# Cached attention in a decoder trunk: values behind the first query block, the merge in four parts, query copies shared, a residual load moved

## The chip, the cores and the metric

The kernel runs on one core of a Trainium2 chip. The metric is the device time of one execution in microseconds (us). Five engines work side by side, each through its own instructions in a fixed order: TensorE (PE, matrix products; its weight loads are listed as PEld), VectorE (DVE), ScalarE (ACT), GpSimd (POOL) and SyncE (SP), which issues transfers. Transfers are also issued from ACT and POOL. Engines wait for each other through semaphores.

## The reference, cut to what matters

The program is one inference step of a two-layer decoder: 1024 new prompt tokens and 8 sample tokens, one for each cached sequence. Layer 0 mixes with an mLSTM, layer 1 with latent attention of 8 heads, and each layer ends in a SwiGLU network. The change lies in layer 1's attention and in the output projection behind it.

```python
def mla_attend_prompt(q_lat, q_rope, c_kv, k_r):          # 1024 tokens, causal
    ...
        s = einsum('bqhc,bkc->bhqk', ql, c_kv) + einsum('bqhr,bkr->bhqk', qr, k_r)
        s = where(kpos <= qpos, s * MLA_SCALE, -inf)
        p = softmax(s)
        return einsum('bhqk,bkc->bqhc', p, c_kv)

def mla_attend_sample(...):                               # 8 sequences, 8192 cached rows each
    c_all = concatenate([cache_latent[layer_idx, pages].reshape(past, KV_LORA), cn])
    kr_all = concatenate([cache_k_rope[layer_idx, pages].reshape(past, QK_ROPE), krn])
    s = einsum('qhc,kc->hqk', ql, c_all) + einsum('qhr,kr->hqk', qr, kr_all)
    p = softmax(s * MLA_SCALE)
    return einsum('hqk,kc->qhc', p, c_all)
```

A cached row has 256 latent and 64 rotary float32 values; the pages lie scattered, and a table gives their order. After the attention comes the output projection, `hp + y @ w_o`, the sum of squares of the result, and the next network.

## The kernel before, in words

All products are float32, made of three products of split operands (high x high, high x low, low x high).

**Order of the work.** The kernel is written as a program for a planner that runs ahead of time. Each instruction has a priority from its place in the program; the planner walks through a cost model's time and gives each engine, among the instructions that its model says are ready, the one of highest priority. What it decides is a fixed order for each engine. `high_priority(offset=SOON)` moves instructions ahead in that choice, and `issue_after(x)` says that instructions of x's engine stand behind x in its order; it is a lower limit, and nothing else is tied by it. On the chip, an engine that reaches an instruction whose operands are missing stands still, with all behind it.

**Attention** (`attention`, from L1594). There are 32 slots: 8 heads by 4 groups G of 256 query rows. In a slot `prompt(h, G)` works on two query blocks of 128 rows. For each block it makes the scores in banks `sc` (L1697 to L1702), ends with a product that adds the causal mask (L1704), takes the maximum (L1705), the exponentials (L1714) and the scaling (L1719). Then, for both blocks, come the transposes of the probabilities (L1737), their split, and the products with the values (L1757), and the result is copied to `ot` (L1760) and stored (L1762). `head_ops` makes the next head's keys and values between the slots; its key products are tied behind `self.qk`, the last mask product.

**The samples' stream** runs beside it. After most slots one unit of `sample_units` is written: a unit gathers 2048 cached rows with indirect transfers on POOL's queue (L1849 into `nat`, four buffers; L1850 into `nrp`, two), transposes them on DVE (L1857) and makes scores (L1864). Two units are a half of a sequence; 16 halves are 8 sequences. After the second unit come maximum, exponentials, a transpose, and 16 copies of the probabilities into `pz` (L1885), eight on DVE and eight on ACT. The rest of the half is the function `values` (L1888), stored in `self.due`: 64 products of the probabilities with the gathered rows (L1893), which free the two `nat` buffers, and the update of the accumulator `acc` (L1894). After a sequence's second half it also merges the 16 partial results of each head: a transpose of the maxima (L1898), a maximum and a broadcast (L1900, L1902), a product that spreads it (L1903), factors (L1905, L1906, L1907), a product that adds up the sums (L1908), weights (L1910, L1912) and the products that give the output (L1914, L1915). The next slot's `prompt` calls it in one go, between its softmax and its transposes, and the 64 products are tied behind `self.qk`, the mask product of the second block.

**The samples' queries** (`sample_query`, L1552) are made once, ahead of the stream: 16 copies of 32x128 on ACT (L1574) and eight of 32x64 on DVE (L1576) put them in `qbd`.

**The output projection** (`out_proj`, `op_tile`). Half 0 is 512 tokens, half 1 is 520. For each half eight tiles d of 128 outputs are made from 24 products; the residual X is added (L871), squared on ACT, and the squares are summed in SS, on POOL for d = 1 to 6 and on DVE for d = 7 (L877). A tile's weights are loaded on SP's queue (L142) and split on ACT and DVE (L117, L118). `op_residual` loads a half of the residual as eight transfers (L843): half 0 on SP's queue ahead of the tiles, half 1 on POOL's queue behind tile d = 0.

Of the kernel before, what the change touches and what calls it, by code (L numbers as in the profile page):

```python
# [13 lines left out]
ALU = mybir.AluOpType  # L14
# [4 lines left out]
P = 128  # L19
D = 1024  # L20
KT = D // P
# [70 lines left out]
class Kern:  # L92
# [764 lines left out]
    def op_tile(self, i, d, tags, early=None):  # L857
# [5 lines left out]
        for cs in OPC[i]:  # L863
# [8 lines left out]
            if d == 0:  # L872
                nc.scalar.activation(SS[:, cs], x, AF.Square)
            else:
                sq = self.t(self.sq[i], [P, 512], "sq")[:, :m]
                nc.scalar.activation(sq, x, AF.Square)  # L876
                (V if d == KT - 1 else nc.gpsimd).tensor_tensor(SS[:, cs], SS[:, cs], sq, op=ALU.add)  # L877
# [3 lines left out]
    def out_proj(self, layer):  # L881
# [672 lines left out]
    def sample_query(self, tq, wT):  # L1554
# [16 lines left out]
        for kb in range(4):  # L1571
            d = qbd[32 * kb:32 * kb + 32, :, :, 8 * kb:8 * kb + 8]
            for cq in range(4):
                nc.scalar.copy(d[:, :, cq:8:4], ql[32 * cq:32 * cq + 32].rearrange("p f (h b) -> p b f h", b=NS))  # L1574
# [19 lines left out]
    def attention(self, ckh, ckl, kk, kl, cqp, cq):  # L1594
# [17 lines left out]
        self.due = None  # L1612
# [59 lines left out]
        def prompt(h, G, kt, vt):  # L1672
# [10 lines left out]
            for i in (2 * G, 2 * G + 1):  # L1683
# [8 lines left out]
                for c in range(nb):  # L1692
# [10 lines left out]
                    if last:  # L1703
                        self.qk = mm(o[:, w - P:], mk[:, 0], mk[:, 1], start=False, stop=True).ins  # L1704
# [18 lines left out]
            if self.due:  # L1723
                self.due()
            for j0 in range(0, nk, 4):
# [3 lines left out]
                for j2 in range(0, m, 2):  # L1729
# [3 lines left out]
                    for jj in range(2):  # L1733
                        for i in range(2):
                            if diag and jj == 1 and i == 0:
                                continue
                            nc.tensor.transpose(ps[:, jj, i * P:(i + 1) * P], pn[i][:, (j + jj) * P:(j + jj + 1) * P], self.ident)  # L1737
# [40 lines left out]
        for h in range(8):  # L1778
# [11 lines left out]
            for i, G in enumerate(range(4) if h % 2 == 0 or h == 7 else range(3, -1, -1)):  # L1790
# [8 lines left out]
                if slot == 30:  # L1799
                    next(units, None)  # L1800
                    if self.due:
                        self.due()
# [19 lines left out]
    def sample_units(self, b, first):  # L1822
# [6 lines left out]
        if self.due:  # L1829
            self.due()  # L1830
# [57 lines left out]
        def values():  # L1888
            self.due = None
# [5 lines left out]
            if not first:  # L1895
                m = t([P, 1], "m", 1)
                V.tensor_scalar(m, nb, -1.0, None, op0=ALU.mult)
                nc.tensor.transpose(ss[0:1, 0:P], m, self.ident)  # L1898
# [4 lines left out]
                nc.tensor.matmul(ss[:, P:P + 1], mc.rearrange("o x h -> o (x h)"), self.ones[0:1, 0:1], start=True, stop=True)  # L1903
# [4 lines left out]
                nc.tensor.matmul(ss[:, 256:257], self.ct[:, C_SL:C_SL + P], lrow, start=True, stop=True)  # L1908
# [4 lines left out]
                for f in range(2):  # L1913
                    nc.tensor.matmul(ss[:, 384 + f * 8:392 + f * 8], acc[:, f * P:(f + 1) * P], w, start=True, stop=True)  # L1914
# [167 lines left out]
```

## Time and profile before

| | us |
|---|---|
| median of three runs | 2600.45 (2599.62 to 2604.7) |
| profiled execution | 2597.15 |
| its span | 2595.3 |
| PE busy | 2492.7 (96%) |
| DVE busy | 1859.5 (72%) |
| ACT busy | 1328.1 (51%) |
| POOL busy | 573.6 (22%) |
| attention with the samples' stream | about 1330 to 1800 |
| output projection of layer 1 | about 1798 to 1903 |

Times in the profile count from the span's start. A group row gives line, engine, operation, tiles and shapes. A wait row reads: engine, tile and line that waited, what ended the wait, then the total in us, the number of waits and the longest. A timeline row gives start and duration in us, and in brackets the idle time of the engine ahead of it with what ended it; an engine name with a trailing q is its queue. A stretch's row gives its length, the busy time of each engine with the number of instructions, the granted clock of TensorE as a share of full speed, the share of the transfer engines and GB/s.

### The profile page before, as it was taken

How to read it: one execution, taken by the hardware profiler on the slowest of the kernel's cores; microseconds unless marked ns; L12 is line 12 of the kernel's file. 1: busy time of each engine (PE TensorE's matmuls, PEld its weight loads, DVE VectorE, ACT ScalarE, POOL GpSimd, SP SyncE). 2: the span in 40 equal slices, each digit the busy share in tenths (PEclk: the TensorE clock that was granted, in tenths of full speed). 3: DMA queues.
4: the chain of work that ended last, by engine and by line, in shares of the span. 5: the costliest groups of instructions: out<-in, count | busy, mean ns of one | idle time of the engine just before them, and what ended most of it. 6: DMA issues, size and time to landing. Idle time of an engine off the chain costs nothing.

```text
span 2595.3 us, 54269 instructions
## 1 busy us (share of the span) xinstructions
PE 2492.7 (96%) x21151; PEld 2360.5 (91%) x21151; DVE 1859.5 (72%) x4491; ACT 1328.1 (51%) x3281; POOL 573.6 (22%) x588
## 2 busy tenths in 40 slices
PE   8998988999999999999988898999999999999998
PEld 8998987999999999999986767777899999999998
DVE  4345669898777777766658777778498877777765
ACT  4122334456655556554454555656256656556643
POOL 1000102301111111112435555542211111111102
PEclk9999999999999999999988999999999999999999
DMA  5123545526566666555467676664535666665663
GB/s 194 42 63 85 151 143 123 162 75 135 117 129 128 127 126 120 111 151 172 157 241 282 232 250 236 222 242 152 192 106 114 119 127 128 130 129 115 120 136 118
DMA packets 343127, 382.87 MB, mean 148 GB/s; under 512 B 23465, under 2 KB 275502, under 8 KB 334550
## 3 DMA queue, kind: packets, MB, share of 16 engines
q0 software_dynamic: 58688, 180.35, 29.9%
q1 hardware_dynamic: 258982, 182.30, 23.7%
q10 hardware_dynamic: 25200, 16.75, 2.4%
q8 instruction: 166, 2.72, 0.4%
q14 instruction: 91, 0.75, 0.1%
HBM read 253.63 MB, written 125.70 MB: 146 GB/s over the span
## 4 chain that ended last, share of the span: by engine, by line
PE 69%; DVE 9%; DMA 6%; issue 2%; ACT 2%; POOL 2%; SPq 0%; ACTq 0%; POOLq 0%; DVEq 0%
PE sc L134 13%; PE sc L136 13%; PE sc L135 13%; PE mm L134 5%; PE mm L136 5%; PE mm L135 5%; DMA nat<-in_cache_latent_dram,idx 2%; PE ss L134 2%; PE ss L135 2%; PE ss L136 2%; DVE tt L1857 2%; PE ss L1864 2%; PE ss L1893 1%; DVE wl L118 1%; PE mm L1757 1%
## 5 line engine op out<-in xcount | busy, mean ns | idle before, releaser
L1187 POOL DMA_DIRECT2D x_d<-wl x72 | 86.8, 1205 | 996.8 <-DVE wl L1186 359.3
L117 ACT ACTIVATE wh<-wr 128x512 fp32r<-128x512 f32 (+2 forms) x167 | 133.5, 800 | 193.8 <-PE mm L135 114.4
L1857 DVE STREAM_TRANSPOSE tt<-nat 128x1024 f32<-128x1024 f32 x128 | 155.4, 1228 | 28.9 <-DMA nat<-in_cache_latent_dram,idx 24.3
L118 DVE TENSOR_TENSOR wl<-wr,wh 128x1024 fp32r<-128x1024 f32 (+2 forms) x80 | 92.5, 1158 | 37.6 <-ACT wh L117 36.2
L134 PE MATMUL mm<-zh,wh 128*128 128x344 f32 x320 | 104.1, 325 | 6.1 <-DVE ot L467 6.1
L117 ACT ACTIVATE b<-u 128x256 fp32r<-128x256 f32 (+1 forms) x252 | 98.5, 415 | 20.4 <-PE ss L136 6.3
L118 DVE TENSOR_TENSOR b<-u,b 128x256 fp32r<-128x256 f32 (+1 forms) x252 | 102.9, 422 | 6.8 <-ACT b L117 5.4
L1187 POOL DMA_DIRECT2D x_d<-st x72 | 105.0, 1459 | 4.2 <-DVE dC L118 3.8
L136 PE MATMUL mm<-zh,wl 128*128 128x344 f32 x320 | 103.7, 324 | 0.0
L135 PE MATMUL mm<-zl,wh 128*128 128x344 f32 x320 | 103.7, 324 | 0.0
L118 DVE TENSOR_TENSOR wh<-S,wh 128x512 fp32r<-128x512 f32 x108 | 74.5, 689 | 34.6 <-ACT wh L117 34.3
L1864 PE MATMUL ss<-tt,qbd 128*32 128x128 f32 x2560 | 88.1, 280 | 10.9 <-DVE tt L1857 8.9
L1864 PEld LDWEIGHTS ss<-tt,qbd 128*32 128x32 f32 x2560 | 70.5, 112 | 26.4 <-DVE tt L1857 18.5
L117 ACT ACTIVATE wh<-S 128x512 fp32r<-128x512 f32 x108 | 67.9, 629 | 44.3 <-PE sc L136 32.1
L134 PE MATMUL sc<-zh,wh 128*128 128x344 f32 x256 | 82.8, 324 | 0.2 <-DVE q L432 0.2
L1757 PE MATMUL mm<-wh,vt 128*128 128x256 f32 (+1 forms) x320 | 74.7, 297 | 8.4 <-ACT wh L117 7.1
L136 PE MATMUL sc<-zh,wl 128*128 128x344 f32 x256 | 82.1, 321 | 0.2 <-DVE wl L118 0.2
L135 PE MATMUL sc<-zl,wh 128*128 128x344 f32 x256 | 82.1, 321 | 0.0
L1714 ACT ACTIVATE wr<-sc,mx,rqt 128x512 f32<-128x512 f32 (+2 forms) x96 | 64.5, 676 | 30.1 <-DVE mx L1709 14.9
L1850 POOL DMA_INDIRECT nrp<-in_cache_k_rope_dram,idx x64 | 61.4, 959 | 57.9 <-DVE tt L1857 24.5
L877 POOL TENSOR_TENSOR ss<-ss,sq 128x512 f32<-128x512 f32 (+2 forms) x36 | 50.7, 1407 | 106.0 <-ACT sq L876 106.0
L1757 PEld LDWEIGHTS mm<-wh,vt 128*128 128x128 f32 x320 | 56.0, 198 | 18.1 <-ACT wh L117 11.2
(1078 smaller groups left out, 10659.1 us busy)
## 6 DMA issues: line engine op xcount, KB each, us to landing
wr<-in_ffn_w_gate_up_dram SPq DMA_DIRECT2D x96, 512.0 KB
x_d<-st POOLq DMA_DIRECT2D x72, 520.0 KB, 7.8
x_d<-wl POOLq DMA_DIRECT2D x72, 512.0 KB, 5.9
dr<-in_ffn_w_down_dram SPq DMA_DIRECT2D x72, 256.0 KB
wr<-in_mlstm_w_in_dram SPq DMA_DIRECT2D x24, 512.0 KB
wr<-in_mlstm_w_out_dram SPq DMA_DIRECT2D x16, 512.0 KB
q<-qn_d SPq DMA_DIRECT2D x28, 256.0 KB
wr<-in_mla_w_o_dram SPq DMA_DIRECT2D x14, 512.0 KB
```

Source lines behind the costliest of these rows:

```text
L117: ins = nc.scalar.activation(hi, src, AF.Copy)
L118: self.low = e.tensor_tensor(lo, src, hi.bitcast(F32), op=ALU.subtract)
L134: mm(ps, wh, xh, start=start, stop=False, **kw)
L135: mm(ps, wh, xl, start=False, stop=False, **kw)
L136: self.last = mm(ps, wl, xh, start=False, stop=stop, **kw)
L877: (V if d == KT - 1 else nc.gpsimd).tensor_tensor(SS[:, cs], SS[:, cs], sq, op=ALU.add)
L1187: nc.gpsimd.dma_start(self.x_d[:, 2 * dp:2 * dp + 2, 512 * i:512 * i + 2 * PW[i]], st[i], accum_op=ALU.add)
L1714: nc.scalar.activation(px[:, ks], o, AF.Exp, bias=mx[:, 0:1], scale=f, accum_out=sm[:, c:c + 1])
L1757: nc.tensor.matmul(o, x, y, start=i == 0, stop=i == len(ops) - 1)
L1850: nc.gpsimd.indirect_dma_start(out=nrp[:, s].rearrange("p s c -> p (s c)"), out_offset=None, in_=rop, in_offset=ix)
L1857: V.transpose(out=tt, in_=src.rearrange("p s (c i) -> p c s i", i=32))
L1864: nc.tensor.matmul(psS[32 * j:32 * j + 32, u * P:u * P + P], self.qbd[:, b, cb], tt[:, c, 4 * j:4 * j + 4].rearrange("p s k -> p (s k)"), ...
```

## The change

It has three parts. First, `values` becomes a generator of four pieces: `prompt` runs one behind the softmax, one ahead of the products with the values, one in the middle of them, and what is left at their end. `self.qk` is now the mask product of the first block of a slot. The pieces' PE steps are tied behind that mark, behind the last transpose, behind the middle product and behind the last product. Where a unit starts with a generator still open, it is run to its end at once. Second, every other of the 16 query copies goes to DVE. Third, the residual's half 1 is loaded behind tile d = 3 in place of d = 0, and its transfers are tied behind POOL's sum of that tile.

```diff
-                (V if d == KT - 1 else nc.gpsimd).tensor_tensor(SS[:, cs], SS[:, cs], sq, op=ALU.add)
+                self.sqa = (V if d == KT - 1 else nc.gpsimd).tensor_tensor(SS[:, cs], SS[:, cs], sq, op=ALU.add)
...
-                if d == 0:
-                    self.op_residual(1, nc.gpsimd)
+                if d == 3:
+                    with self.tc.issue_after(self.sqa.ins):
+                        self.op_residual(1, nc.gpsimd)
...
-                nc.scalar.copy(d[:, :, cq:8:4], ql[32 * cq:32 * cq + 32].rearrange("p f (h b) -> p b f h", b=NS))
+                (nc.scalar.copy, V.tensor_copy)[cq % 2](d[:, :, cq:8:4], ql[32 * cq:32 * cq + 32].rearrange("p f (h b) -> p b f h", b=NS))
...
-                        self.qk = mm(o[:, w - P:], mk[:, 0], mk[:, 1], start=False, stop=True).ins
+                        qk = mm(o[:, w - P:], mk[:, 0], mk[:, 1], start=False, stop=True).ins
+                        self.qk = qk if i % 2 == 0 else self.qk
...
-            if self.due:
-                self.due()
+            next(self.due, None)
...
-                            nc.tensor.transpose(ps[:, jj, i * P:(i + 1) * P], ...)
+                            self.tn = nc.tensor.transpose(ps[:, jj, i * P:(i + 1) * P], ...)
...
+            next(self.due, None)
             for i, (o, x, y) in enumerate(ops):
-                nc.tensor.matmul(o, x, y, start=i == 0, stop=i == len(ops) - 1)
+                self.pv = nc.tensor.matmul(o, x, y, start=i == 0, stop=i == len(ops) - 1)
+                if i == len(ops) // 2:
+                    next(self.due, None)
+            drain(self.due)
...
         def values():
-            self.due = None
...
             if not first:
                 m = t([P, 1], "m", 1)
                 V.tensor_scalar(m, nb, -1.0, None, op0=ALU.mult)
-                nc.tensor.transpose(ss[0:1, 0:P], m, self.ident)
+                with self.tc.high_priority(offset=SOON), self.tc.issue_after(self.qk):
+                    nc.tensor.transpose(ss[0:1, 0:P], m, self.ident)
+                yield
...
-                nc.tensor.matmul(ss[:, P:P + 1], mc.rearrange("o x h -> o (x h)"), self.ones[0:1, 0:1], start=True, stop=True)
+                with self.tc.issue_after(self.tn.ins):
+                    nc.tensor.matmul(ss[:, P:P + 1], mc.rearrange("o x h -> o (x h)"), self.ones[0:1, 0:1], start=True, stop=True)
+                yield
...
-                nc.tensor.matmul(ss[:, 256:257], self.ct[:, C_SL:C_SL + P], lrow, start=True, stop=True)
+                with self.tc.issue_after(self.pv.ins):
+                    nc.tensor.matmul(ss[:, 256:257], self.ct[:, C_SL:C_SL + P], lrow, start=True, stop=True)
+                yield
...
-                for f in range(2):
-                    nc.tensor.matmul(ss[:, 384 + f * 8:392 + f * 8], acc[:, f * P:(f + 1) * P], w, start=True, stop=True)
+                with self.tc.issue_after(self.pv.ins):
+                    for f in range(2):
+                        nc.tensor.matmul(ss[:, 384 + f * 8:392 + f * 8], acc[:, f * P:(f + 1) * P], w, start=True, stop=True)
...
-        self.due = values
+        self.due = values()
```

More of the change, by code (lines that the diff above doesn't have):

```diff
@@ L1611, in attention @@
         ahead = {}
-        self.due = None
+        self.due = iter(())
         def load_q(h, G):
@@ L1736, in prompt @@
                                 continue
[L1737 removed]
+                            self.tn = nc.tensor.transpose(ps[:, jj, i * P:(i + 1) * P], pn[i][:, (j + jj) * P:(j + jj + 1) * P], self.ident)
                     if diag:
@@ L1800, in attention @@
                     next(units, None)
-                    if self.due:
-                        self.due()
+                    drain(self.due)
                     pr.release()
@@ L1828, in sample_units @@
         rop = self.cache_k_rope.rearrange("l n (r s) c -> (l n r) (s c)", s=8)
-        if self.due:
-            self.due()
+        for _ in self.due:
+            pass
         if first:
```

1 line of the change is left out of this document (removed).

## The prediction

> **What bounds the kernel now.** I read the page's first part, then a table of busy time over stretches, then who waited for whom inside the stretch that the change touches.
>
> ```profile
> PE 2492.7 (96%) x21151; PEld 2360.5 (91%) x21151; DVE 1859.5 (72%) x4491; ACT 1328.1 (51%) x3281; POOL 573.6 (22%) x588
> ...
> core 0: us, PE busy (x) PEld busy (x) DVE busy (x) ACT busy (x) POOL busy (x), PEclk, DMA share, GB/s
> 1330.00:1800.00 470.00, 418.34 (x5245) 335.02 (x5245) 351.10 (x782) 268.13 (x705) 221.32 (x219) 0.95 0.67 233
> ...
> 1475.90:1479.30 3.40, 3.40 (x16) 3.24 (x15) 3.40 (x10) 1.22 (x5) 0.00 (x0) 0.50 0.98 387
> 1837.70:1841.10 3.40, 2.91 (x7) 2.15 (x7) 2.36 (x3) 1.69 (x2) 1.38 (x1) 0.50 0.31 90
> ```
>
> TensorE (PE) is the bound: 96% busy. It leaves 102.6 us of the span, and half of that, 470 - 418.3 = 51.7 us, lies in 1330 to 1800, the cached attention that the change edits. VectorE (DVE) is busy 351 of 470 us there, so it is no second bound. The last two rows show what a pause costs besides itself: 3.4 us at half the granted clock (0.50), each behind a pause of some three microseconds (both are quoted below as waits of 3.0 and 3.11). Half of 3.4 us, 1.7 us, is lost each time.
>
> ```profile
> PE ss L1864 <- DVE tt L1857: 8.9, 7, 2.6
> ...
> PE sc L1697 <- ACT wr L1714: 6.6, 4, 5.5
> PE ss L1903 <- DVE sS L1902: 5.4, 4, 3.0
> PE mm L134 <- ACT ot L1760: 4.7, 2, 2.6
> ...
> PE mm L1737 <- ACT wr L1719: 2.2, 5, 1.1
> PE ss L1914 <- DVE w L1912: 1.8, 3, 0.8
> PE ss L1903 <- DVE tt L1857: 1.3, 1, 1.3
> ```
>
> These are PE's waits in that stretch (total us, times, longest). The pauses are many and small. Those of the merge (L1903, L1914) sum to 8.5 us.
>
> **Part A, the second residual half.** The eight POOL loads of 260 KB go from behind tile d=0 to behind POOL's sum of tile d=3.
>
> ```profile
> 1827.11 8.81 DMA wr<-in_mla_w_o_dram
> ...
> 1817.75 4.34 POOL L843 DMA_DIRECT2D x<-x_d  x8 [5.03 <-DVE wl L118]
> 1829.94 1.29 POOL L877 TENSOR_TENSOR ss<-ss,sq 128x512 f32<-128x512 f32 x1 [1.18 <-ACT sq L876]
> ...
> 1837.12 0.50 PE L134 MATMUL mm<-zh0h,wh 128*128 128x512 f32 x1 [3.11 <-ACT wh L117]
> 1838.38 0.79 PE L136 MATMUL mm<-zh0h,wl 128*128 128x512 f32 x1 [0.49 <-DVE wl L118]
> 1855.76 0.28 PE L134 MATMUL mm<-zh1h,wh 128*128 128x256 f32 x1
> ...
> DMA packets 5678, 6.95 MB, mean 289 GB/s; under 512 B 368, under 2 KB 3630, under 8 KB 5678
> q0 software_dynamic: 640, 2.13, 23.4%
> ```
>
> The weights of tile d=5 take 8.81 us to land, and PE stands 3.11 + 0.49 = 3.6 us, then runs at half clock (1.7): 5.3 us. The last two rows are of 1816 to 1840: 6.95 MB went through, of which POOL's queue, the second residual half, was 2.13 MB, or 7.4 us at the mean 289 GB/s. Without it ahead, the weights land some 5 us earlier and the stall goes. The moved loads leave after POOL's fourth row, at about 1831, take 4.3 us to issue, and are first needed when PE finishes the tile begun at 1855.76: over 20 us of cover. Late next could be the weights of d=6, asked for just then: at worst their stall replaces this one (gain 0). Nothing that POOL does then waits behind the new wait except its sums of d=4 to d=6, and issuing cost them 4.34 us at the old place as well. Bounds: 0 to 5.3; being nearest to the upper row, I take **4.5**.
>
> **Part C, query copies.** Eight of sixteen copies leave ScalarE (ACT) for DVE.
>
> ```profile
> L1574 ACT COPY qbd<-ql x16: 413/416/428, 1338.6 to 1347.2; 32x128 f32<-32x128 f32 x16
> L1576 DVE COPY qbd<-qrS x8: 208/215/420, 1321.8 to 1325.3; 32x64 f32<-32x64 f32 x8
> L1885 DVE COPY pz<-pT x128: 140/186/1296, 1383.4 to 1779.2; 32x64 f32<-32x64 f32 x128
> ...
> 1348.65 0.67 ACT L1714 ACTIVATE wr<-sc,mx,rqt 128x384 f32<-128x384 f32 x1 [1.04 <-issue]
> 1349.44 0.16 DVE L1717 RECIPROCAL sm<-sm 128x1 f32<-128x1 f32 x1 [6.10 <-ACT wr L1714]
> 1353.43 1.29 POOL L130 TENSOR_TENSOR wl<-spl,wh 128x512 fp32r<-128x512 f32 x1 [13.99 <-ACT spl L129]
> 1354.88 0.98 POOL L1850 DMA_INDIRECT nrp<-in_cache_k_rope_dram,idx  x1 [0.15 <-DVE mx L1709]
> ```
>
> The exponentials at 1348.65 wait behind the copies on ACT; PE waits 5.5 us for them (the first L1697 row above), and POOL stands 14 us on ACT's split with the next gather queued behind it. Eight copies off ACT are 8 x 0.416 = 3.3 us. On DVE a copy of twice the elements of L1576 costs 0.19 to 0.43 us, so at most 3.4 us, under DVE's 6.1 us of idling at the same place. PE's wait, ACT's split and the gather all move up by 3.3. Bounds: the worst DVE copy of the rows is 1.296 us, and eight of those, 10.4 us, would outlast the 6.1 by 4.3 (a loss of 4.3); at the other end stand 5.0 gained (3.3 and one half-clock stretch). The median row being the nearest, I take **3.3**.
>
> L1885's row, 186 ns at the median and 1296 at the most, shows that DVE's copies are now and then held up for a microsecond. The Trainium skill, "SBUF — State Buffer", section "SBUF: two separate sides", names a cause that would work both ways: an fp32 copy within SBUF on VectorE and GpSimd's accesses exclude each other at a shared port, and GpSimd cannot write the descriptors of its own DMAs meanwhile. The trace agrees as far as the copies go; no row here shows a gather held up. By that rule part C would be 0 and the sum 11.2, by the row it is 3.3 and 14.5.
>
> **Part B, values and merge.** The value products (L1893) were ordered behind the second query block's last score product; now behind the first's. The merge's four PE steps, once issued in one go, are tied behind the scores, the transposes, the middle and the end of the prompt's value products.
>
> ```profile
> 1454.80 0.24 ACT L1885 COPY pz<-pT 32x64 f32<-32x64 f32 x1
> 1460.45 0.85 PE L1893 MATMUL ss<-nat,pz 128*32 128x256 f32 x12
> ...
> 1526.26 0.38 PE L1903 MATMUL ss<-ones,sS 1*128 1x1 f32 x2 [1.07 <-DVE sS L1902]
> ...
> 1701.79 0.24 ACT L1885 COPY pz<-pT 32x64 f32<-32x64 f32 x1
> 1702.04 0.22 PE L1704 MATMUL sc<-mk 128*128 128x128 f32 x1
> ...
> 1712.43 0.31 PE L1704 MATMUL sc<-mk 128*128 128x128 f32 x1
> 1712.67 3.66 PE L1893 MATMUL ss<-nat,pz 128*32 128x256 f32 x64
> 1716.11 0.96 POOL L1849 DMA_INDIRECT nat<-in_cache_latent_dram,idx  x1 [0.16 <-issue]
> ...
> 1738.91 0.22 PE L1704 MATMUL sc<-mk 128*128 128x128 f32 x1
> 1743.78 0.42 PE L1893 MATMUL ss<-nat,pz 128*32 128x256 f32 x4
> ...
> DVE tt L1857 <- DMA nat<-in_cache_latent_dram,idx: 24.3, 10, 6.6
> POOL nat L1849 <- PE ss L1893: 13.5, 6, 6.4
> POOL acc L1833 <- PE ss L1914: 6.8, 3, 3.0
> ```
>
> In the group at 1712 the last copy of the probabilities ends at 1702.03 and the first block's last product at 1702.26; the values start at 1712.67, right after the second block's. So 10.4 us are free to be taken, and the gather that refills the freed buffers goes out only at 1716.11. Ten of the sixteen groups are held so, by 1.8 to 10.4 us; the first (copies done at 1455.04, values at 1460.45) and the last (first block done at 1739.13, values at 1743.78) stand in the fence. The last three rows say why it matters: POOL waits 13.5 us for these products before gathering, and DVE then waits 24.3 us for the data, which reaches PE as the 8.9 us of L1864.
>
> - Merge waits: 8.5, of which the merge behind slot 11 (the row at 1526, 1.07), where two units follow each other with no prompt between them, stays in one go. Of the 7.4 left I take two thirds, **5.0**; bounds 0 to 9 with one half-clock stretch.
> - Earlier gathers: of L1864's 8.9, 2.6 are the very first gather, so 6.3 can go; the waits for the prompt's store (ot, 4.7) may go too if the store no longer meets the burst of gathers. I take half of the 11.0, **5.7** with a little clock; bounds 0 to 14.4 (both whole, and two half-clock stretches).
> - Lost cover: the 3.66 us of values ran while the second block's softmax was made. PE already waits 2.2 us for that (L1737). Scores of the cache and products of the next head can fill in, but not always: **-4.0**, bounds 0 to -36.6 (ten groups, nothing fills).
> - The next head's key products hang on the same mark and are freed too: no instruction more, fillers for the pauses. I cost them at nothing; badly placed they are part of the lost cover.
> - Queue: POOL's clear of the accumulator waits for the last merge product (6.8 us, three times), now tied behind the prompt's last value product; gathers and POOL's splits queue behind it. I put it inside the -4.0.
>
> Sum of B: **6.7**. A + B + C = 14.5. The profiled execution took 2597.15 (span 2595.3 and 1.85 around it), 3.3 under the median 2600.45; it would become 2582.65, the median **2586**.
>
> **The rivals.**
> 1. *Lost cover decides* (slower). Place: between the second block's mask product and its transposes. At 1712.43 the values gave 3.66 us; if other work fills only 1.5 of it, PE loses 2.16 x 10 = 21.6 us. The gathers bring nothing then, as their data is no longer what is waited for, and 12.8 of A, C and the merge remain: 8.8 slower, 2609. It decides once more than 1.3 us a group (12.8 / 10) stays open. For: the 2.2 us row. Against: PE had fillers ready around 1716 (cache scores), and the planner places values by when it reckons them ready.
> 2. *Nothing measurable.* The pauses move rather than go: C is eaten by the wait for the first gather (2.6 us of L1864), the merge's waits reappear at the tied places, and of A some 3.5 stays: 2597.
> 3. *All of it goes.* A 5.3, C 5.0, merge 7.4, half of the rest 7.3: 25 faster, 2575.
> 4. *The change doesn't do what it says.* The tie is a lower limit only; if the planner still places the values after the second block, B gives nothing: 14.5 - 6.7 = 7.8, 2592.6.
> 5. *DVE's copies hold up POOL's gathers*: eight copies of 0.43 us are 3.4 us in which the gathers at 1335 to 1355 could not be issued, as much as ACT gains, so C is 0: 2589.3. For: the 1296 ns. Against: POOL stood idle for 14 us there, so there was little to hold up. The Trainium skill's "SBUF — State Buffer" has this rule, as said under part C.
>
> **How the numbers follow.** Forecast 0.43, rival 1 0.12, 2 0.16, 3 0.12, 4 0.12, 5 0.05. A difference of 0.2% is 5.2 us. Faster: 0.43 + 0.12 + 0.12 + 0.05 = 0.72; same 0.16; slower 0.12. The range holds rivals 2 to 5 with their scatter and stops short of rival 1's centre: 2573 to 2606. The forecast's own case alone spans 2580 to 2591.
>
> **What would show it.** A: the pause before tile d=5 is gone and that stretch has full clock. C: ACT's exponentials near 1348 start 3 us earlier, with DVE's eight copies at 0.2 to 0.43 us. B: value products start after an odd-numbered mask product with the second block's scores behind them; waits on L1902 and L1912 fall under 2 us together; DVE's 24.3 us on the gathers falls by half. I am wrong if PE's waits for L1719 or L117 grow by more than 10 us, if the stretch from 1330 to 1800 is not shorter by at least 5 us, or if the weights of d=6 inherit the stall.

## The result, and the profile after

The changed kernel takes **2634.14 us** (median, 2629.25 to 2636.95); the kernel before, measured beside it, 2601.81. The ratio is **1.0123** [1.0103, 1.0142]: 32 us slower, where 15 us faster was forecast. The profiled execution took 2631.37 us, with a span of 2629.6.

The first part of the page after, and the stretch of the cached attention (columns as before):

```profile
PE 2505.1 (95%) x21151; PEld 2371.1 (90%) x21151; DVE 1859.5 (71%) x4499; ACT 1322.2 (50%) x3273; POOL 573.5 (22%) x588
```

```profile
1330.00:1800.00 470.00, 400.73 (x4888) 321.44 (x4887) 320.36 (x719) 241.34 (x634) 218.93 (x216) 0.91 0.65 228
```

PE executes the same 21151 products. In the same 470 us it got through 4888 of them instead of 5245; its pauses grew from 51.7 to 69.3 us, and the granted clock fell from 0.95 to 0.91. Since the count is equal, the start of the n-th product after can be set against that of the n-th before (times below are those before). The profiled run after is already 4.3 us late when the attention begins, though nothing is changed there; some 4 us ahead in slot 11, at 1519; 14 late at 1603, 23 at 1665, 39 at 1800; and 33.4 late from 1890 to the end. So the loss lies in slots 12 to 31, where prompt slots and cache units run side by side. PE's waits after, in 1325 to 1850:

```profile
PE ss L1868 <- DVE tt L1861: 17.0, 10, 5.1
PE sc L1698 <- DMA q<-qn_d: 13.6, 5, 6.9
PE mm L1738 <- ACT wr L1721: 12.7, 6, 5.0
...
PE sc L1698 <- ACT wr L1716: 3.9, 5, 1.7
PE sc L134 <- ACT zh0h L117: 3.7, 1, 3.7
```

The merge's 8.5 us are off the list, and L1698's wait for the exponentials fell from 6.6 to 3.9. In their place the cache scores wait for transposed keys 17.0 us (8.9 before, L1864), the transposes for scaled probabilities 12.7 (2.2 before, L1737), and the scores for the prompt's queries 13.6, which was no wait at all before. VectorE's waits in the same stretch:

```profile
DVE tt L1861 <- DMA nat<-in_cache_latent_dram,idx: 32.1, 10, 8.3
DVE fac L1912 <- PE ss L1909: 23.2, 6, 9.2
...
DVE rl L1919 <- PE ss L1916: 9.1, 5, 3.9
```

The wait for gathers did not halve; it rose from 24.3 to 32.1. The merge's waits have moved to VectorE (23.2 for the spread product), where the transposes of the next keys queue behind them. PE around slot 21, after:

```profile
1686.49 0.28 PE L1705 MATMUL sc<-mk 128*128 128x128 f32 x1
1686.70 3.66 PE L1896 MATMUL ss<-nat,pz 128*32 128x256 f32 x64
1690.29 0.50 PE L1698 MATMUL sc<-kt,q 128*128 128x512 f32 x1
...
1692.15 0.23 PE L1705 MATMUL sc<-mk 128*128 128x128 f32 x1
...
1694.60 0.22 PE L1705 MATMUL sc<-mk 128*128 128x128 f32 x1
1701.69 0.45 PE L1698 MATMUL sc<-kt,q 128*128 128x128 f32 x1 [6.87 <-DMA q<-qn_d]
```

The change does what it says: the 64 value products stand right behind the first block's mask product, and slot 21's second block is scored after them (its mask product at 1692.15). Slot 22's scores follow at once (1694.60). Slot 23's queries can only be loaded into the buffer that slot 21 has just left, so PE stands 6.87 us. Before, the second blocks' mask products of slots 21 and 22 ended 18 us apart (1662.0 and 1680.4); here 2.4.

### The profile page after: what moved, and what is told of

Same layout as the page of the kernel before. It is cut to its first block, busy times and chain, and to the rows that moved or that the text cites. A ratio compares the mean times of both kernels' runs of the same rounds, so it can differ in the third digit from the quotient of the medians.

```text
span 2629.6 us, 54288 instructions
## 1 busy us (share of the span) xinstructions
PE 2505.1 (95%) x21151; PEld 2371.1 (90%) x21151; DVE 1859.5 (71%) x4499; ACT 1322.2 (50%) x3273; POOL 573.5 (22%) x588
## 4 chain that ended last, share of the span: by engine, by line
PE 63%; DVE 10%; DMA 7%; issue 4%; ACT 2%; POOL 2%; SPq 0%; ACTq 0%; POOLq 0%; DVEq 0%
PE sc L136 12%; PE sc L134 12%; PE sc L135 12%; PE mm L134 4%; PE mm L136 4%; PE mm L135 4%; DMA nat<-in_cache_latent_dram,idx 2%; DVE tt L1861 2%; PE ss L134 2%; PE ss L136 2%; PE ss L135 2%; PE ss L1896 1%; DVE wl L118 1%; PE mm L1759 1%; PE ss L1868 1%
## 5 line engine op out<-in xcount | busy, mean ns | idle before, releaser
L1861 DVE STREAM_TRANSPOSE tt<-nat 128x1024 f32<-128x1024 f32 x128 | 153.9, 1223 | 33.8 <-DMA nat<-in_cache_latent_dram,idx 32.1
L118 DVE TENSOR_TENSOR wl<-wr,wh 128x1024 fp32r<-128x1024 f32 (+2 forms) x80 | 92.6, 1160 | 32.1 <-ACT wh L117 31.7
L1868 PEld LDWEIGHTS ss<-tt,qbd 128*32 128x32 f32 x2560 | 71.0, 113 | 33.7 <-DVE tt L1861 26.0
L1716 ACT ACTIVATE wr<-sc,mx,rqt 128x512 f32<-128x512 f32 (+2 forms) x96 | 64.3, 675 | 44.7 <-DVE mx L1711 24.3
L130 POOL TENSOR_TENSOR wl<-spl,wh 128x512 fp32r<-128x512 f32 x43 | 54.6, 1280 | 88.2 <-ACT spl L129 56.8
```

The source lines that it names most:

```text
L118: self.low = e.tensor_tensor(lo, src, hi.bitcast(F32), op=ALU.subtract)
L130: nc.gpsimd.tensor_tensor(lo, x, hi.bitcast(F32), op=ALU.subtract)
L1716: nc.scalar.activation(px[:, ks], o, AF.Exp, bias=mx[:, 0:1], scale=f, accum_out=sm[:, c:c + 1])
L1861: V.transpose(out=tt, in_=src.rearrange("p s (c i) -> p c s i", i=32))
L1868: nc.tensor.matmul(psS[32 * j:32 * j + 32, u * P:u * P + P], self.qbd[:, b, cb], tt[:, c, 4 * j:4 * j + 4].rearrange("p s k -> p (s k)"), ...
```

## The experiments

A ratio is to the kernel before, run beside it in the same group. In the group of e10, e12 and e16 the kernel before took 2612.03 us, in the others 2595 to 2602; why is open, so medians are compared only within a group. Letters for theories are those of each expectation's own text.

| kernel | ratio [95%] | median, us |
|---|---|---|
| the change | 1.0123 [1.0103, 1.0142] | 2634.14 |
| mark alone (e2) | 1.0118 [1.0088, 1.0148] | 2632.0 |
| merge in parts alone (e3) | 1.0059 [1.0034, 1.0083] | 2613.63 |
| residual half and copies (e4) | 0.9965 [0.9952, 0.9978] | 2587.95 |
| the change, row in its own place (e1) | 1.0067 [1.0048, 1.0086] | 2618.61 |
| merge in parts, own row (e8) | 0.9977 [0.9962, 0.9991] | 2590.89 |
| value products' mark alone (e6) | 1.0162 [1.0136, 1.0187] | 2635.88 |
| key products' mark alone (e7) | 1.0014 [1.0, 1.0028] | 2599.71 |
| half of the value products (e15) | 1.009 [1.0071, 1.0109] | 2618.69 |
| gathers freed, second mark (e13) | 0.9918 [0.9901, 0.9935] | 2576.31 |
| gathers freed, first mark (e14) | 0.9963 [0.9947, 0.9979] | 2588.68 |
| as e6, no priority (e16) | 1.0032 [1.0013, 1.0051] | 2619.92 |
| the change, no priority (e17) | 1.0064 [1.0039, 1.0089] | 2620.38 |
| the change, no priority, own row (e18) | 1.0018 [0.9999, 1.0037] | 2605.93 |
| all but the mark, own row (e11) | 0.9989 [0.9976, 1.0002] | 2592.04 |
| residual half alone (e9) | 0.9986 [0.9972, 1.0001] | 2592.5 |
| copies alone (e10) | 0.9998 [0.9981, 1.0015] | 2611.92 |
| half, copies, own row (e12) | 0.9974 [0.9959, 0.999] | 2607.37 |

### Which part loses

Three kernels each take a part of the change alone. The mark (e2):

```diff
-                        self.qk = mm(o[:, w - P:], mk[:, 0], mk[:, 1], start=False, stop=True).ins
+                        qk = mm(o[:, w - P:], mk[:, 0], mk[:, 1], start=False, stop=True).ins
+                        self.qk = qk if i % 2 == 0 else self.qk
```

> The kernel before, with only the mark moved: values and the next head's key products behind the first block's mask product, the merge in one go and untied, residual and copies as before. S and H: no loss, 2592 to 2604. C: most of the loss, 2615 to 2635.

The merge as a generator of four tied pieces, as in the change's diff, with the mark at the second block (e3):

> The kernel before, with only the merge in four tied parts, the mark still the second block's mask product. S and H: most of the loss, 2620 to 2637. C: none, 2592 to 2604, with the merge's waits on L1902 and L1912 of 8.5 us gone.

The residual's half behind d = 3 and every second query copy on VectorE, the first two pieces of the change's diff (e4):

> The kernel before, with only the residual half moved and half of the query copies on VectorE, attention as before. All theories: 2591 to 2597; part A was put at 4.5 us and part C at 3.3. If the copies gain nothing, 2595 to 2598.

Measured: +1.18%, +0.59%, -0.35%. The sum, 1.42, is close to the change's 1.23. So two parts lose by themselves, and the part that the prediction had as a mere addition gains. Two of the three times lie outside every range set for them: the merge in parts (2613.63) loses less than S and H said, and the residual's half with the copies (2587.95) gains more than any theory gave it.

### The merge's row and the buffer it takes

The merge spreads its maxima through a row `mc`, which is cut from the tile "sS". That tile has one buffer, and the next half's exponentials are written to it. Here the row lives in a small tile that is no longer used, in the change (e1) and in the kernel with the merge in parts alone (e8):

```diff
-                mc = t([P, 256], "sS", 1)[0:1, :P].rearrange("o (x h) -> o x h", h=8)
+                mc = self.gn[0:1].rearrange("o (x h) -> o x h", h=8)
```

> The changed kernel, with the merge's row of maxima in a place of its own instead of the one buffer that the next half's exponentials use. Theory S (shared buffer: the row is held until a product that is now tied behind the prompt's last transpose, so the next half's exponentials start 17 to 27 us after its scores): that delay falls under 15 us in every half and the time to 2590 to 2605. Theory C (lost cover: the values no longer run during the second block's softmax): unchanged, 2625 to 2637. Theory H (VectorE stands at the factor of the merge, 23 us, behind the tied product): 2615 to 2637, the 23 us remain.

> The kernel before, with the merge in four tied parts at the second block's mark (that edit alone cost 15 us), and the merge's row in a place of its own, so that it no longer holds the one buffer of the next half's exponentials. Theory S: the shared buffer is the whole cost of the parts. S expects 2595 to 2602, the merge's PE waits of 7.4 us gone and the delay from the cache scores to the exponentials back at 9 to 15 us. Rival T: the ties themselves cost, since the merge's DVE operations now stand in VectorE's order before the next half's transposes and wait there for PE. T expects 2608 to 2615.

The half at 1567 to 1607 shows the buffer. Before (the last cache scores of the half, the spread product that reads the row, the exponentials):

```profile
1567.68 1.08 PE L1864 MATMUL ss<-tt,qbd 128*32 128x128 f32 x32
...
1583.75 0.38 PE L1903 MATMUL ss<-ones,sS 1*128 1x1 f32 x2 [0.69 <-DVE sS L1902]
...
1584.17 0.47 ACT L1877 ACTIVATE sS<-ss,nb 128x256 f32<-128x256 f32 x1
```

The same three after:

```profile
1578.96 1.08 PE L1868 MATMUL ss<-tt,qbd 128*32 128x128 f32 x32
...
1605.08 0.38 PE L1909 MATMUL ss<-ones,sS 1*128 1x1 f32 x2
...
1607.15 0.51 ACT L1881 ACTIVATE sS<-ss,nb 128x256 f32<-128x256 f32 x1
```

And with the merge in parts and the row in its own place:

```profile
1574.12 1.08 PE L1866 MATMUL ss<-tt,qbd 128*32 128x128 f32 x32
...
1577.12 0.49 ACT L1879 ACTIVATE sS<-ss,nb 128x256 f32<-128x256 f32 x1
```

Scores to exponentials: 1584.17 - 1568.76 = 15.4 us before, 27.1 after, 1.9 with its own row. Over the seven halves that follow a merge the mean is 9.6 us before, 12.6 with the merge in parts alone (e3), 18.8 in the change, 1.9 in e8 and 1.7 in e1. The exponentials had been waiting for the row already before; drawing the merge out made it worse. With its own row the merge in parts goes from +0.59% to -0.23%, so S holds for the parts: the shared buffer is what they cost, and the ties cost nothing that shows on top.

In the whole change the same edit brings 0.56 points, and 0.67 stay. The time of e1, 2618.61, misses S's range and lies in H's. VectorE's wait at the merge's factor indeed stays there, at 26.4 us, and no run takes away that wait alone; but the mark alone (e2) loses 1.18% with 7.4 us of it. PE's wait for keys is back at 9.0 us in e1, as before; its waits for the prompt's queries (11.5, none before) and for scaled probabilities (6.5, 2.2 before) are what stands out.

### What the early mark does

The mark moves two things, the cache's value products and the next head's key products. One kernel moves only the first (e6), one only the second (e7):

```diff
+                        self.q1 = self.qk if i % 2 == 0 else self.q1
...
-            with self.tc.high_priority(offset=SOON), self.tc.issue_after(self.qk):
+            with self.tc.high_priority(offset=SOON), self.tc.issue_after(self.q1):
```

> The kernel before, with one edit: the cache's value products wait for the first query block's mask product, as in the change, while the next head's key products still wait for the second block's, as before. (In the change and in the run with the mark alone, one mark moved both.) Theory V: the value products, 64 instructions in 3.7 us at high priority, now stand between the two blocks' scores, so that the second block's scores, its maximum, its exponentials and its scaling start later and nothing is left to cover them. V expects most of the 33 us that the mark alone cost: 2620 to 2635. Theory K: the key products, 12 products of 512 columns for each half of the columns, were freed by the same mark and are what is put ahead of the second block's scores. K expects 2590 to 2603 here.

> The kernel before, with the reverse edit: the next head's key products wait for the first query block's mask product, the cache's value products for the second block's, as before. Theory V expects no loss: 2590 to 2605. Theory K expects most of the 33 us: 2620 to 2635. If both this run and its twin lose about half, the mark acts on both.

It is the value products: +1.62%, against +0.14% for the key products. K falls. But V's mechanism is not what the waits of e6 show. PE's waits in it:

```profile
PE ss L1865 <- DVE tt L1858: 22.4, 14, 5.0
PE sc L1697 <- DMA q<-qn_d: 9.7, 5, 3.2
PE sc L1697 <- ACT wr L1715: 9.4, 6, 5.0
PE mm L1758 <- ACT wh L117: 8.0, 11, 1.8
...
PE mm L1738 <- ACT wr L1720: 2.1, 3, 1.2
```

The transposes wait for the second block's probabilities no longer than before (2.1 against 2.2). It is the cache scores that wait: 22.4 against 8.9. The trace tells how long a gather's way is. From the end of a half's value products, which free the gathers' buffers, to the end of the fourth transpose, the last of the first unit's keys fetched into them, pass 17.3 us before, 19.8 in e6 and 23.5 in the change (means over 12 halves). The first 9.2, 9.4 and 9.4 of that are the gather's flight. What grows is the stretch of VectorE's transposes behind it: 8.1, 10.4 and 14.1 us, with 4.9 us of the four transposes' own work in each. VectorE in such a stretch, before (`acc` marks the end of the value products):

```profile
1603.90 0.48 DVE L1894 SCALAR_TENSOR_TENSOR acc<-acc,al,ss 128x256 f32<-128x256 f32 x1 [0.37 <-issue]
...
1612.22 1.34 DVE L1885 COPY pz<-pT 32x64 f32<-32x64 f32 x6
1613.59 1.25 DVE L1857 STREAM_TRANSPOSE tt<-nat 128x1024 f32<-128x1024 f32 x1
...
1618.15 1.25 DVE L1857 STREAM_TRANSPOSE tt<-nat 128x1024 f32<-128x1024 f32 x1 [0.88 <-PE ss L1864]
```

And in e6:

```profile
1602.90 0.48 DVE L1895 SCALAR_TENSOR_TENSOR acc<-acc,al,ss 128x256 f32<-128x256 f32 x1 [0.62 <-issue]
...
1611.14 1.25 DVE L1858 STREAM_TRANSPOSE tt<-nat 128x1024 f32<-128x1024 f32 x1 [1.71 <-DMA nat<-in_cache_latent_dram,idx]
...
1614.05 0.56 DVE L1886 COPY pz<-pT 32x64 f32<-32x64 f32 x3
1614.63 0.69 DVE L1706 TENSOR_REDUCE mx<-sc 128x1 f32<-128x512 f32 x1
1615.34 0.99 DVE L1886 COPY pz<-pT 32x64 f32<-32x64 f32 x5
1616.34 1.25 DVE L1858 STREAM_TRANSPOSE tt<-nat 128x1024 f32<-128x1024 f32 x1
...
1620.76 0.69 DVE L1706 TENSOR_REDUCE mx<-sc 128x1 f32<-128x512 f32 x1 [2.17 <-PE sc L1702]
...
1621.56 2.36 DVE L1858 STREAM_TRANSPOSE tt<-nat 128x1024 f32<-128x1024 f32 x2
```

Before, the second block was scored ahead of the value products, so that the gather's flight was left for the next slot's first block and the other half's placing copies; VectorE was through with both at 1613.6, and the four transposes took 5.8 us. In e6 the flight goes to the second block, and what stood there before comes into the stretch of transposes: the next slot's maxima and the placing copies fall between them, VectorE even stands 2.17 us for a score product ahead of transposes whose data landed at 1611, and the four take 12.8 us. Over the 12 stretches VectorE's maxima rose from 10.2 to 15.5 us and its placing copies from 10.4 to 19.3.

Some of these copies are also slow. The longest wait of e6, 4.98 us, with VectorE and POOL ahead of it:

```profile
1528.14 3.08 DVE L1886 COPY pz<-pT 32x64 f32<-32x64 f32 x2
1531.52 2.04 DVE L1886 COPY pz<-pT 32x64 f32<-32x64 f32 x5
1533.60 1.25 DVE L1858 STREAM_TRANSPOSE tt<-nat 128x1024 f32<-128x1024 f32 x1
...
1528.44 2.53 POOL L130 TENSOR_TENSOR wl<-spl,wh 128x512 fp32r<-128x512 f32 x2
1531.65 1.26 POOL L130 TENSOR_TENSOR wl<-spl,wh 128x512 fp32r<-128x512 f32 x1 [0.68 <-ACT spl L129]
...
1534.90 1.94 PE L1865 MATMUL ss<-tt,qbd 128*32 128x128 f32 x32 [4.98 <-DVE tt L1858]
```

Such a copy takes VectorE 0.19 us at the median. The five that take it over half a microsecond before, and the eight in e6, all end within 0.1 us behind such a split on POOL; ScalarE's placing copies never take more than 0.25 us. So VectorE's copies are held up by POOL's splits, and in e6 the order of the work brings more of them together. All 128 copies take 33.7 us of VectorE in e6, 29.9 before, so this is a part of the loss, not the whole.

Set product by product against the kernel before, e6 is 8.7 us ahead at 1519, within 5 us of it from 1537 to 1620, and 36 us behind at 1790. The early mark gains in the first slots and loses in the later ones.

If the gather's way is what costs, the mark should be nearly free when gathers need not wait for the value products. In the next two kernels the value products read a constant tile instead of the gathered keys (the cache's part of the output is left out so), and a gather's buffer is free once the transposes have read it; mark at the second block (e13) and the first (e14):

```diff
-                        nc.tensor.matmul(psV[32 * j:32 * j + 32], pz[:, j, i], keys[i // 4][:, j * 4 + i % 4], start=i == 0, stop=i == 7)
+                        nc.tensor.matmul(psV[32 * j:32 * j + 32], pz[:, j, i], self.ct[:, C_SL:C_SL + 256], start=i == 0, stop=i == 7)
```

> The kernel before, but the cache's value products read a constant tile of the same shape in place of the gathered keys (the cache's part of the output is left out in that way: the same 64 products, other numbers). So a gather's buffer comes free when its transposes have read it, and the next gathers no longer wait for the value products. Mark at the second block, as before. Theory G: the loss of the early mark is in the round trip value products, gather, transposes, cache scores, which in the run with the values' mark alone took 22.7 us from the end of the value products to the last cache score of the half after next, 18.6 before (mean of 12 halves), with PE idle 55.6 us in it, 32.0 before. G expects this run well below the kernel before, since the 24 us that VectorE waits for gathers and the 9 us that PE waits for transposes go: 2565 to 2590. Theory V (cover for the second block's softmax) expects little: 2585 to 2600.

> As its twin (the value products read a constant tile, gathers don't wait for them), with the value products at the first block's mark. G expects the mark to cost little now, the two within 10 us of each other. V expects the 40 us of the values' mark again, or most of it, since the value products still stand ahead of the second block's scores: 25 to 45 us above its twin. In between (10 to 25): both take part.

The mark now costs 12.4 us between the medians (2588.68 - 2576.31) instead of 40. By this comparison both take part, the gather's way with some 28 of the 40. VectorE's waits for gathers are gone in both. PE's wait for keys, 8.9 us before, stays, though G expected it to go. In the second-mark and in the first-mark kernel it is:

```profile
PE ss L1864 <- DVE tt L1857: 9.9, 17, 1.8
```

```profile
PE ss L1865 <- DVE tt L1858: 14.1, 15, 1.9
```

With only the first unit's 32 value products at the early mark (e15):

```diff
-            with self.tc.high_priority(offset=SOON), self.tc.issue_after(self.qk):
-                for i in range(8):
+            for i in range(8):
+                with self.tc.high_priority(offset=SOON), self.tc.issue_after(self.q1 if i < 4 else self.qk):
```

> The kernel before, with the value products cut in two: the 32 of the first gathered unit wait for the first block's mask product, the 32 of the second unit for the second block's, as before. V, a loss by what stands ahead of the second block's scores, expects half of the 40 us: 2612 to 2622. G expects less or a gain: the first gather's buffer comes free earlier and only 1.8 us go ahead of the second block: 2585 to 2610. A planned order that jumps from one to the other gives all of it: 2625 or more.

+0.90%, a good half of +1.62%: the loss goes with what is put ahead, as V had it, and earlier freedom of the first gather's buffer does not make up for it, as G had it.

Last, the value products of e6 without their priority (e16):

```diff
-            with self.tc.high_priority(offset=SOON), self.tc.issue_after(self.q1):
+            with self.tc.issue_after(self.q1):
```

> As the run with the values' mark alone (value products allowed from the first block's mask product on, key products from the second's), but without the high priority of the value products: they may start as early, and are no longer put ahead of the second block's scores. If the loss comes from their standing ahead (12 us of the 40 that stayed when the gathers no longer waited for them, and the second block's maxima between the gathered keys' transposes), it goes to a good part: 2595 to 2615. If it comes from any start before the second block's mark, it stays: 2625 to 2640. Later value products would also delay the next gathers, which can add a loss of its own: above 2640.

```profile
1330.00:1800.00 470.00, 412.71 (x5070) 315.58 (x5069) 332.07 (x727) 253.62 (x656) 218.31 (x215) 0.95 0.66 225
```

```profile
PE ss L1865 <- DVE tt L1858: 14.7, 12, 4.0
```

+0.32%: four fifths of the loss are gone (a rough figure, as it sets two groups side by side), the clock is back at 0.95, the wait for the prompt's queries is off the list, and the stretch of transposes takes 7.7 us (10.4 in e6). The planner now spreads the 64 products over 4 to 14 us among other work; in 14 of 16 halves they start behind the second block after all. So the run shows that the priority put them where they cost; it does not show what an early start that is well spread would be worth.

The gather's way is thus no measure of the time by itself. It is 23.7 us in e1, as long as in the change, at half the loss, and 18.5 in e8, longer than before, in a faster kernel. Nor is PE's wait for keys, the largest in e17 (24.6 us) at +0.64%. That the way makes most of the mark's loss rests on e13 and e14.

### Both causes taken out of the change

The change without the priority (e17), and so with the row's own place as in e1 (e18):

```diff
-            with self.tc.high_priority(offset=SOON), self.tc.issue_after(self.qk):
+            with self.tc.issue_after(self.qk):
                 for i in range(8):
```

> The whole change, with one edit: the value products without high priority. Taken alone, the values' mark cost 1.62% and only 0.32% without the priority. If that is also what costs in the change (1.23%), some 1.0 to 1.3 points go: a ratio of 0.998 to 1.004 to the kernel before. If in the change the drawn-out merge with the shared row buffer still delays the next half's exponentials, more stays: 1.004 to 1.009.

> The whole change, with both: the value products without high priority, and the merge's row in a place of its own (which alone brought the change from 1.0123 to 1.0067). If the two causes are all of the loss, what is left is the gain of the residual's half and the copies, 0.9965, and perhaps some of the merge's: a ratio of 0.993 to 0.998. If a third cause is in it: 0.999 or more.

In the change itself the priority is worth 0.59 points (1.0123 to 1.0064), about half of what the mark's own runs had led to expect, and priority and row together 1.05 (to 1.0018). VectorE's wait for the merge's spread product, 23.2 us, is 3.5 without the priority. The two causes are thus most of the loss, but not all: with the gain of the other two parts 0.9965 would be left, and 0.53 points above that stay unexplained (the early start without priority, 0.32 by itself, may be most of it).

### The parts that gain

Of the change's diff, e9 keeps only the residual's half, e10 only the query copies, e12 both, with the merge's row in its own place and the merge in one go. e11 is the change with the row's own place and this:

```diff
-                        self.qk = qk if i % 2 == 0 else self.qk
+                        self.qk = qk
```

> The kernel before, with the residual's second half moved behind d = 3 and nothing else. The prediction gave it 4.5 us and the query copies 3.3; the two together measured 11. If the half alone is that: 2588; by the prediction's size 2591 to 2593, with the pause of 3.1 us before d = 5 gone; if the half does nothing and the copies all, 2596 to 2600.

> The kernel before, with the query copies shared between ScalarE and VectorE and nothing else. The prediction gave this 3.3 us, from the 8 copies of 0.416 us that leave ScalarE; the half alone measured 3 us, the two together 9 to 11. Sizes as predicted: 2591 to 2593. If the two simply add up: 2587 to 2590. If they only gain together: 2594 to 2598.

> The kernel before with the residual's half later and the query copies shared (the two parts that gained), and the merge's row in a place of its own, the merge in one go as before. If the shared buffer also costs the merge in one go, 2 to 5 us below the run without it: 2583 to 2587. If the row matters only when the merge is drawn out over a slot: 2586 to 2591. If a new planned order takes the gain back, as when all the gaining parts were put together: 2591 to 2596.

> The whole change, except that the mark stays at the second block's mask product, and with the merge's row in a place of its own: the residual's half later, the query copies shared, the merge in four parts. From the runs of the parts: 11 us gained by the half and the copies, and what the four parts cost without the shared buffer. S (parts cost nothing then) expects 2584 to 2590; T (the ties cost some 10) 2596 to 2603; if the parts gain the 5 us of the merge's waits that the prediction gave them, 2580 to 2585.

The residual's half alone does what was said. The rows of the kernel before and of e9 for 1800 to 1840:

```profile
1800.00:1840.00 40.00, 36.12 (x162) 28.65 (x161) 20.43 (x33) 16.65 (x36) 12.15 (x17) 0.93 0.69 224
```

```profile
1800.00:1840.00 40.00, 39.74 (x188) 32.90 (x188) 24.45 (x45) 21.13 (x50) 13.56 (x18) 0.91 0.71 220
```

PE's pauses there fall from 3.9 to 0.3 us, and the time by 0.14%, 3.6 us [-7.3, +0.3]. The copies alone change nothing that can be measured, though PE's longest wait behind them falls from 5.5 to 1.7, in e10:

```profile
PE sc L1697 <- ACT wr L1714: 2.7, 3, 1.7
```

Both together are 0.9965, the fastest kernel of the study that leaves nothing out, ahead of the kernel before and of the change. The gains don't add up: half and copies (-0.35%) and the merge in parts with its own row (-0.23%) give -0.11% together (e11), and an own row on top of half and copies gives nothing that can be measured (e12), though the exponentials' delay behind a merge falls to 4.8 us there. PE's wait for keys is 15.0 us in e11, 9.4 in e4 and 11.0 in e8. Each edit makes the planner lay out the whole attention anew; why this layout comes out worse was not settled.

## Why the prediction was wrong

**Part B, earlier gathers (5.7): the step that failed.** It read 10.4 us between the copies of the probabilities and the value products as time to be taken, and let gathers, transposes and scores move up with them. The value products do start behind the first block, but that mark itself comes later: in slot 13 it ends at 1548.5 after, where before even the second block's had ended at 1541.5. Only up to slot 11 did the early mark gain (e6 is 8.7 us ahead there). The 24.3 us that were to halve became 32.1. What was missed is VectorE's share of the way behind the gather, 8.1 us before and 14.1 after for the same 4.9 us of transposes: before, they went through quickly because the next slot's first block and the placing copies were done while the gather flew. The merge in parts lengthens that stretch further, with the row in its own place too (14.0 us in e1, 10.4 in e6 without the parts). How the 0.67% that stay in e1 divide was not settled. The step asked who waits for the data, not what else its receiver will be doing when it lands.

**Part B, lost cover (-4.0, bounds 0 to -36.6).** The sign was right. e6 loses 40 us between the medians, close to the far bound, but by coincidence, as the place was wrong for the most part. The step saw 3.66 us of PE work that covered PE's wait for the softmax; in e6 that wait did not grow (2.1), and in the change it did (12.7). What lost its place in the gather's flight was the next block's work on VectorE. Rival 1 had the right side with 8.8 us and a chance of 0.12; one sign of being wrong that the prediction named, PE waiting over 10 us more for L1719 (now L1721), was met in the change, 12.7 against 2.2. The prediction's reason against it, that the planner puts the value products where it reckons them ready, overlooked their high priority: that is what put them ahead (1.62% with it, 0.32% without; 1.23% and 0.64% in the change).

**Part B, merge (5.0).** The waits went as predicted, and with the row in a place of its own the parts bring 0.23%, 6.0 us [-9.9, -2.3]. The step looked at PE's waits only and did not ask which buffers the merge holds while it is drawn out: the row's, for which the next half's exponentials wait. That turned the gain into 15 us of loss.

**Part B, POOL's queue (inside the -4.0).** The clear of the accumulator waits 33.9 us after, 6.8 before. It waits 23.7 in e8 too, which is faster than the kernel before, so this wait by itself was not what cost. It is 30.2 in e6, with the merge in one go, so the early mark lengthens it as well.

**Part B, key products (nothing).** Right: +0.14% [0, 0.28].

**Part A (4.5).** Right in mechanism and, as far as it can be measured, in size: 3.6 us with an interval that just reaches zero, the pause before d = 5 gone in e9 and in the change (PE is busy 60.00 of the 60 us from 1840 to 1900 there). In the change PE pauses 3.7 us at the start of the projection instead (the last wait row of the list after, zh0h); e9, with the merge in one go, has no such pause, and e8 and e11, with the merge in parts, have one of 3.5; but e3, in parts too, has none, so its cause is open. The weights of d = 6 did not inherit the stall.

**Part C (3.3).** The copies went as said: eight on VectorE at 265 to 419 ns, and the 5.5 us wait became at most 1.7. Counted from the copy that makes `ql`, the exponentials come 2.3 us sooner in e10, 3.5 in e4 and 3.7 in the change. But `ql` itself was ready 2.7 to 4.5 us later in these runs than before, so that the exponentials start at 1349.19, 1347.90 and 1349.43, against 1348.65; why it was later is open. The gain did not follow: 0.9998 alone, which is what rivals 2 and 5 said, together with A 0.9965 where 7.8 us, 0.9970, were predicted. Rival 5's reason, POOL's gathers held up by the copies, does not show in the trace. POOL and VectorE at that place in e4:

```profile
1337.87 1.15 POOL L1850 DMA_INDIRECT nat<-in_cache_latent_dram,idx  x1 [0.17 <-issue]
...
1339.90 1.02 POOL L1851 DMA_INDIRECT nrp<-in_cache_k_rope_dram,idx  x1 [0.30 <-issue]
```

```profile
1337.81 2.42 DVE L1575 COPY qbd<-ql 32x128 f32<-32x128 f32 x8
```

One gather is issued wholly and one begins while VectorE copies, in 1.15 and 1.02 us; before, without the copies, it was 1.07 and 1.02. The rule of the Trainium skill that was weighed there ("SBUF — State Buffer", "SBUF: two separate sides") would have kept POOL out for as long as a copy in a two-port mode lasts. The profile does not say whether these copies run in that mode; it shows no such hold-up of POOL. The opposite one it does show: VectorE's placing copies wait for POOL's splits, as seen in e6, and the 1296 ns of the prediction's row are such a wait.

## What to carry to other kernels

Before work is moved ahead of other work, ask for every engine, not only for the bound, what will run when the moved work's consumer is released: here data landed just when the receiving engine had been given something else. When a chain is cut into tied pieces, list what it holds while it is drawn out, the single buffers first. And where a planner orders the work, take a priority away before an early mark is blamed or praised: it decided some four fifths of what the mark cost alone, and half of what the change cost.

## What the runs showed of the hardware

A copy of 32x128 took 0.27 us on VectorE (eight in 2.42 us, back to back) and 0.42 on ScalarE. VectorE's copies of 32x64, 0.19 us at the median, took up to 1.30 us before and 2.89 in e6 when a split of 128x512 on POOL ran beside them, and ended with it; none of them on ScalarE took more than 0.25.

In the 470 us of the attention the mean granted clock was 0.95 with 51.7 us of pauses before and 0.91 with 69.3 after, so the pauses cost more than their length. Their sum alone does not give the clock: it was 0.92 in e12 with 49.3 us.

The profiles of e10, e12 and e16 show waits that the others lack, such as 24 short ones before the cache scores that end in nothing the profile shows (e10):

```profile
PE ss L1864 <- issue: 9.9, 24, 1.0
```

What causes them is open.
